# Start of a four-layer encoder: first loads in pieces of two tiles, and the squares moved behind the first value splits

## The chip, the cores and the metric

One NeuronCore of a Trainium2 chip runs the whole kernel in one launch. The metric is the device time of the launch in microseconds (us). The other cores do nothing.

## What is computed

A trunk of four layers (an even mixer, an MLP, an odd mixer, an MLP) over 256 tokens of width 1024, all in float32. Only the start of the even layer is touched by this change:

```python
def rms_norm(x, g):
    xf = x.astype(jnp.float32)
    y = xf * lax.rsqrt(jnp.mean(xf * xf, axis=-1, keepdims=True) + RMS_EPS)
    return (y * g.astype(jnp.float32)).astype(x.dtype)

xn = rms_norm(x, norm_mix[layer])
hcat = xn @ w_in                                  # 1024 -> 1952
a_qkv = hcat[..., :o0]                            # o0 = 1536: q, k, v, 512 columns each
c_q, c_kv, k_pe = 256, 128 and 32 further columns # 416 columns in all: "c" below
```

## The kernel before

`x` lies transposed in SBUF as eight tiles of 128 features by 256 tokens. The norm is applied late: the matmuls run on `x` times the gain, and their results are scaled by the reciprocal root mean square `r`, which comes from the squares of `x`. Each float32 operand is split into a high half (rounded, type fp32r) and the rest, and each product is three matmuls: high by high, high by low, low by high (`mm3`, L178).

Weights are listed in `specs` (L105 to L132) in the order of their use. Each is a `raw` tile of 128 partitions, from a pool of four (`RAWBUFS`), and its halves `whi` and `wlo` are a pair from a pool of three (`WBUFS`). `load_weight` (L137) issues a load on SP's queue, in one piece or several; `split_piece` (L152) makes a quarter of the halves, the high one with a copy on ScalarE (L175), the low one with a subtraction on VectorE (L176).

The start of the even layer runs in this order. Eight matmuls on a zero tile (`keep_warm`, L87 to L91) occupy TensorE at first. SP issues, for each k of eight, the tile k of `x` (128 KB) and the quarter of a `w_c` weight that goes with it (208 KB; `w_c` is two weights of four quarters each), then the first `w_v` weight in two pieces, the second in one, and `w_qk` (L474 to L477). The loop at L556 then does for each k: `prepare` (L224), which makes both halves of the gained tile (ScalarE L227, VectorE L228), one `split_piece`, and six matmuls of 416 columns (`c_product`). After every second k, `add_squares` (L230) squares two tiles of `x` on ScalarE (L233) and adds them up on VectorE (L235, in the end L237). Behind the loop stand the four splits of the first `w_v` weight (L569). A second part (L570 to L582) multiplies by `w_v`: `v0` and `v1` are the two token halves, four k of each with the first weight and four with the second, 12 matmuls of 512 columns each time. Between `v0` and `v1`, `rstd` (L248) sums the squares over partitions with small matmuls (L243), and `r`, `diagonal` and `c_tail` follow from it.

Both parts stand in `tc.manual_schedule`: TensorE, ScalarE and VectorE keep the written order there. The DMAs on SP keep the order in which they are written, too, and each takes the next of eight completion semaphores (`DMAHW0` to `DMAHW7` in the order listings); a DMA that takes one in use waits, on SP, until the earlier DMA has landed. `tc.issue_after(i)` puts what its block writes on the engine of the instruction `i` behind `i`; it says nothing to other engines. Behind line 582 a scheduler fills the rest of the even layer in by priorities.

Of the kernel before, what the change touches and what calls it, by code (L numbers as in the profile page):

```python
# [16 lines left out]
F32 = mybir.dt.float32  # L17
# [6 lines left out]
P = 128  # L24
D = 1024
KT = D // P
T = 256
# [7 lines left out]
WCH = 2048  # L35
# [9 lines left out]
def trunk(ctx, tc, a, out):  # L45
# [41 lines left out]
    def keep_warm(n):  # L87
        for _ in range(n):
            nc.tensor.matmul(idle, warm[:, 0:P], warm, start=True, stop=True)

    keep_warm(8)  # L91

    gains = const.tile([P, 4 * KT], F32, name="gains")
    nc.scalar.dma_start(gains, a["gains"])
    ident = const.tile([P, P], F32, name="ident")
# [41 lines left out]
    def load_weight(pieces=1, before=lambda i: None):  # L137
        j = state["loaded"]
        src, n = specs[j]
        raw = wraw.tile([P, WCH], F32, tag="raw", name="raw")  # L140
        for i in range(pieces):
            c = cut(j, i, pieces)
            before(i)
            nc.sync.dma_start(raw[:, c], src[:, c])
        parts[j] = [raw, None, None]
        state["loaded"] = j + 1
# [324 lines left out]
    def even(ep):  # L471
        xT = x_pair()
        xh, xl = halves(xT)
        for j in range(2):  # L474
            load_weight(4, lambda i: nc.sync.dma_start(x[:, 4 * j + i, :], a["x"][:, 4 * j + i, :]))
        load_weight(2)
        load_weight()  # L477
# [77 lines left out]
        with tc.manual_schedule(engines={ENG.PE, ENG.Activation, ENG.DVE}):  # L555
            for k in range(KT):  # L556
                upper, lower = prepare(k, 0, xT)
                upper()
                lower()
                split_piece()  # L560
                if k % 4 == 0:
                    wc.append(parts[k // 4][1:])
                for t in range(NT):
                    c_product(pc[t], wc[k // 4], k, t)
                if k % 2:
                    add_squares(k // 2, s)
            state["used"] = 2
            del parts[0], parts[1]
            ins = [split_piece() for _ in range(WPARTS)][-1]  # L569
        with tc.issue_after(ins[0]), tc.issue_after(ins[1]):  # L570
            with tc.manual_schedule(engines={ENG.PE, ENG.Activation, ENG.DVE}):
                v0, v1 = v_steps(0), v_steps(1)
                v0(range(4))
                small_loads()
                r = rstd(s)
                dg = [diagonal(r, t) for t in range(NT)]
                v1(range(4))
# [413 lines left out]
def _layout(i):  # L991
    f = np.ascontiguousarray
    w = i["ev_w_in"][0]
    d = {"x": f(i["x"][0][ORDER].T.reshape(KT, P, T).transpose(1, 0, 2))}
# [27 lines left out]
    gains = np.stack([i["norm_mix"], i["norm_mlp"]], 1).reshape(4 * KT, P)  # L1022
    d["gains"] = f(gains.T)
# [21 lines left out]
```

## Time and profile before

| what | us |
| --- | --- |
| median of 3 runs (lowest to highest) | 748.24 (748.11 to 748.69) |
| the profiled execution | 748.74 |
| its span, from the first to the last instruction | 747.0 |
| TensorE busy in the span | 736.6 (99%) |
| VectorE busy | 552.1 (74%) |
| ScalarE busy | 466.1 (62%) |

The profiled execution is 0.5 us over the median; 1.74 us of it lie outside the span. TensorE's busy time counts from the start of a matmul to its modelled end, so that matmuls that follow each other closely overlap, and pauses show best in the distance between starts. "PEld" is the load of the stationary operand. An entry such as `[1.78 <-DMA raw<-in_w_c]` says how long the engine had been idle and what released it.

### The profile page before, as it was taken

Reading aid. Unit: us, or ns where it says so; the run is one execution under the profiler, and the core shown is the slowest. Engines: PE = TensorE matmul, PEld = TensorE weight load, DVE = VectorE, ACT = ScalarE, POOL = GpSimd, SP = SyncE. Lnnn points to the kernel's source line nnn. Section 1 sums busy time; section 2 is a strip of 40 time slices with the busy share of each in tenths; the row PEclk is TensorE's granted clock in tenths of the full one; section 3 lists DMA queues with packets and bytes.
Section 4 is the critical chain, followed back from the end, with each engine's and each line's share of the span. In section 5 each row is a group of like instructions: output and inputs, shape, how many; then the busy total and the mean of one; then the engine's idle time right before and its main releaser. Section 6 shows DMA issues by size and latency. Waiting matters only on the chain.

```text
span 747.0 us, 12623 instructions
## 1 busy us (share of the span) xinstructions
PE 736.6 (99%) x4700; PEld 641.9 (86%) x4700; DVE 552.1 (74%) x1270; ACT 466.1 (62%) x1052; POOL 7.6 (1%) x20
## 2 busy tenths in 40 slices
PE   8999999999999999999999999999999999999996
PEld 5887899888888888989899899998998888888885
DVE  6798859766656656898988888888769665665664
ACT  6688887545545446848676867867667554554541
POOL 0100000000000000000000000000000000000000
PEclk9999999999999999999999999999999999999999
DMA  8764333655555554576555556456653655455501
GB/s 287 312 214 154 114 114 113 227 177 183 204 186 183 195 172 154 196 216 201 198 199 163 169 192 216 164 183 202 227 196 127 211 182 190 173 200 184 181 31 57
DMA packets 27421, 135.32 MB, mean 181 GB/s; under 512 B 4448, under 2 KB 7008, under 8 KB 14432
## 3 DMA queue, kind: packets, MB, share of 16 engines
q1 hardware_dynamic: 27072, 134.23, 51.9%
q8 instruction: 37, 0.61, 0.4%
q10 hardware_dynamic: 288, 0.28, 0.1%
q14 instruction: 24, 0.20, 0.1%
HBM read 127.16 MB, written 1.05 MB: 172 GB/s over the span
## 4 chain that ended last, share of the span: by engine, by line
PE 93%; DVE 2%; DMA 1%; ACT 1%; issue 1%; SPq 0%; POOLq 0%; POOL 0%; DVEq 0%
PE w L185 16%; PE acc L185 14%; PE acc L179 13%; PE acc L180 13%; PE acc L181 13%; PE w L186 8%; PE acc L186 7%; PE w L895 1%; PE w L200 1%; PE acc L910 1%; DMA raw<-in_w_v 1%; PE w L709 1%; PE w L724 1%; PE w L874 1%; DMA raw<-in_w_c 1%
## 5 line engine op out<-in xcount | busy, mean ns | idle before, releaser
L176 DVE TENSOR_TENSOR wlo<-raw,whi 128x512 fp32r<-128x512 f32 (+3 forms) x488 | 304.5, 664 | 75.2 <-ACT whi L175 73.7
L175 ACT CAST whi<-raw 128x512 fp32r<-128x512 f32 (+3 forms) x488 | 264.2, 601 | 80.6 <-issue 69.6
L185 PE MATMUL w<-xT,whi 128*128 128x512 f32 x528 | 185.1, 394 | 0.0
L185 PE MATMUL acc<-xT,whi 128*128 128x512 f32 x432 | 155.3, 402 | 0.0
L186 PE MATMUL w<-xT,wlo 128*128 128x256 f32 x528 | 137.0, 280 | 0.0
L185 PEld LDWEIGHTS w<-xT,whi 128*128 128x128 f32 x528 | 96.5, 187 | 18.8
L186 PE MATMUL acc<-xT,wlo 128*128 128x256 f32 x432 | 112.2, 280 | 0.0
L186 PEld LDWEIGHTS w<-xT,wlo 128*128 128x128 f32 x528 | 99.1, 188 | 5.7
L179 PE MATMUL acc<-whi,h 128*128 128x512 f32 x250 | 98.4, 393 | 0.0
L180 PE MATMUL acc<-wlo,h 128*128 128x512 f32 x250 | 97.8, 391 | 0.0
L181 PE MATMUL acc<-whi,h 128*128 128x512 f32 x250 | 97.4, 390 | 0.0
L185 PEld LDWEIGHTS acc<-xT,whi 128*128 128x128 f32 x432 | 78.8, 188 | 14.7
L186 PEld LDWEIGHTS acc<-xT,wlo 128*128 128x128 f32 x432 | 81.2, 188 | 4.0
L192 ACT COPY up<-w 128x256 f32<-128x256 f32 x64 | 23.9, 373 | 88.5 <-PE w L185 88.5
L193 DVE TENSOR_TENSOR up<-up,w 128x256 f32<-128x256 f32 x64 | 26.9, 420 | 62.9 <-ACT up L192 62.3
L179 PE MATMUL acc<-whi,xT 128*128 128x384 f32 (+2 forms) x160 | 56.2, 351 | 1.0 <-ACT whi L175 0.9
L180 PE MATMUL acc<-wlo,xT 128*128 128x384 f32 (+2 forms) x160 | 55.7, 348 | 0.6 <-DVE wlo L176 0.6
L181 PEld LDWEIGHTS acc<-whi,h 128*128 128x128 f32 x250 | 46.9, 188 | 10.2
L180 PEld LDWEIGHTS acc<-wlo,h 128*128 128x128 f32 x250 | 47.0, 188 | 9.8
L181 PE MATMUL acc<-whi,xT 128*128 128x384 f32 (+2 forms) x160 | 55.2, 345 | 0.0
L179 PEld LDWEIGHTS acc<-whi,h 128*128 128x128 f32 x250 | 46.9, 188 | 9.0
L180 PEld LDWEIGHTS acc<-wlo,xT 128*128 128x128 f32 x160 | 30.1, 188 | 3.2 <-DVE wlo L176 2.2
(186 smaller groups left out, 959.3 us busy)
## 6 DMA issues: line engine op xcount, KB each, us to landing
raw<-in_w SPq DMA_DIRECT2D x64, 1024.0 KB, 4.8
raw<-in_w_oqk SPq DMA_DIRECT2D x24, 1024.0 KB, 5.1
raw<-in_w_ov SPq DMA_DIRECT2D x16, 768.0 KB, 4.8
sw<-qk SPq DMA_DIRECT2D x96, 64.0 KB, 3.2
raw<-in_w_qk SPq DMA_DIRECT2D x4, 1024.0 KB, 11.0
raw<-in_w_oe SPq DMA_DIRECT2D x4, 1024.0 KB, 4.9
raw<-in_w_oo SPq DMA_DIRECT2D x4, 1024.0 KB, 5.5
bias<-in_rpb SPq DMA_DIRECT2D x8, 256.0 KB, 4.0
```

Of the source, the lines that this page charges most:

```text
L175: a = nc.scalar.copy(hi, src).ins
L176: return a, (eng or nc.vector).tensor_tensor(lo, src, hi.bitcast(F32), op=ALU.subtract).ins
L179: nc.tensor.matmul(o, sh, mh, start=first, stop=False)
L180: nc.tensor.matmul(o, sh, ml, start=False, stop=False)
L181: nc.tensor.matmul(o, sl, mh, start=False, stop=last)
L185: both = lambda: nc.tensor.matmul(o, sh, m.rearrange("p v n -> p (v n)"), start=first, stop=last)
L186: low = lambda: nc.tensor.matmul(o[:, 0:T], sl, m[:, 0, :], start=False, stop=False)
L192: nc.scalar.copy(dst, o[:, T:2 * T])
L193: nc.vector.tensor_tensor(dst, dst, o[:, 0:T], op=ALU.add)
L200: nc.tensor.matmul(o[j], qk[pb, 0, a, ts], qk[pb, 1, b, :], start=n == 0, stop=n == 2)
L709: nc.tensor.transpose(pt[:, b * P:(b + 1) * P], pp[:, b // 2, (b % 2) * P:(b % 2 + 1) * P], ident)
L724: nc.tensor.matmul(pvo[64 * j:64 * j + 64, tok(t)], v[:, kk, h * 64:(h + 1) * 64], pts[:, 2 * j + kk, :], start=kk == 0, stop=kk == NT - 1)
```

## The change

The first eight pairs of loads become seven loads. Tiles 0 and 1 of `x` come in one DMA (256 KB), then the two quarters of `w_c` for them (416 KB), then the same for tiles 2 and 3, then tiles 4 to 7 in one DMA (512 KB), then the two halves of the second `w_c` weight. The last three stand in an `issue_after` block on the seventh of now nine warm-up matmuls. The loads of the first `w_v` weight stand in `issue_after` blocks on the splits of k = 0 and 1, that of the second on the split of k = 3; `w_qk` is no longer loaded ahead by hand. The squares leave the loop: all four `add_squares` stand behind the four splits of the first `w_v` weight. `rstd` and `diagonal` move behind `v1(range(4))`. The layout of `gains` on the host stands in another place; its values are the same.

```diff
-    keep_warm(8)
+    warmed = keep_warm(9)
...
-    def load_weight(pieces=1, before=lambda i: None):
-        j = state["loaded"]
+    def load_pieces(j, i0, i1):
+
         src, n = specs[j]
-        raw = wraw.tile([P, WCH], F32, tag="raw", name="raw")
-        for i in range(pieces):
-            c = cut(j, i, pieces)
-            before(i)
-            nc.sync.dma_start(raw[:, c], src[:, c])
-        parts[j] = [raw, None, None]
-        state["loaded"] = j + 1
+        if i0 == 0:
+            parts[j] = [wraw.tile([P, WCH], F32, tag="raw", name="raw"), None, None]
+        c = slice(i0 * n // WPARTS, i1 * n // WPARTS)
+        nc.sync.dma_start(parts[j][0][:, c], src[:, c])
...
-        for j in range(2):
-            load_weight(4, lambda i: nc.sync.dma_start(x[:, 4 * j + i, :], a["x"][:, 4 * j + i, :]))
-        load_weight(2)
-        load_weight()
+        for k in (0, 2):
+            load_x(k, k + 2)
+            load_pieces(0, k, k + 2)
+        with tc.issue_after(warmed[6]):
+            load_x(4, 8)
+            load_pieces(1, 0, 2)
+            load_pieces(1, 2, 4)
+
+        def load_behind(k, done):
+
+            with tc.issue_after(done[0]):
+                if k < 2:
+                    load_pieces(2, 2 * k, 2 * k + 2)
+                elif k == 3:
+                    load_pieces(3, 0, WPARTS)
+                    state["loaded"] = 4
...
-                split_piece()
+                load_behind(k, split_piece())
                 if k % 4 == 0:
                     wc.append(parts[k // 4][1:])
                 for t in range(NT):
                     c_product(pc[t], wc[k // 4], k, t)
-                if k % 2:
-                    add_squares(k // 2, s)
...
                 v0, v1 = v_steps(0), v_steps(1)
+                for b in range(4):
+                    add_squares(b, s)
                 v0(range(4))
                 small_loads()
+                v1(range(4))
                 r = rstd(s)
                 dg = [diagonal(r, t) for t in range(NT)]
-                v1(range(4))
```

What the built program holds shows in two places. First SP's queue, from the eighth load on before, and the names of the semaphores that each waits for:

```order
L144 DMA raw<-in_w_c 128x416 [waits DMAHW0_49]
L475 DMA x<-in_x 128x256 [waits DMAHW1_49]
L144 DMA raw<-in_w_c 128x416 [waits DMAHW2_49]
L475 DMA x<-in_x 128x256 [waits DMAHW3_49]
L144 DMA raw<-in_w_c 128x416 [waits DMAHW4_49]
L475 DMA x<-in_x 128x256 [waits DMAHW5_49]
L144 DMA raw<-in_w_c 128x416 [waits DMAHW6_49]
L475 DMA x<-in_x 128x256 [waits DMAHW7_49]
L144 DMA raw<-in_w_v 128x1024 [waits DMAHW1_49]
L144 DMA raw<-in_w_v 128x2048 [waits DMAHW3_49]
L144 DMA raw<-in_w_qk 128x2048 [waits DMAHW4_49,DVE_49]
```

And SP's queue in the changed program, from the third load on:

```order
L96 DMA x<-in_x 128x512
L146 DMA raw<-in_w_c 128x832
L96 DMA x<-in_x 128x1024
L146 DMA raw<-in_w_c 128x832 x2
L146 DMA raw<-in_w_v 128x1024 [waits DMAHW0_49]
L146 DMA raw<-in_w_v 128x1024 [waits DMAHW1_49]
L146 DMA raw<-in_w_v 128x2048 [waits DMAHW2_49]
L146 DMA raw<-in_w_qk 128x2048 [waits DMAHW4_49,DMAHW3_49,DVE_49]
```

All seven loads of `x` and `w_c` now go out without a wait, and the three of `w_v` wait for the landing of the gains and of the first two loads alone. No load of `x`, `w_c` or `w_v` waits for TensorE or ScalarE: the `issue_after` blocks leave nothing on SP.

Second, VectorE from the last two k of the loop to the mean square `ms`, before:

```order
L228 SCALAR_TENSOR_TENSOR xT<-x,gains,xT 128x256
L176 TENSOR_TENSOR wlo<-raw,whi 128x416
L235 TENSOR_TENSOR squares<-squares,q 128x512
L237 TENSOR_TENSOR squares<-squares 128x256
L176 TENSOR_TENSOR wlo<-raw,whi 128x512 x8
L245 TENSOR_SCALAR ms<-w 128x2
```

And in the changed program:

```order
L232 SCALAR_TENSOR_TENSOR xT<-x,gains,xT 128x256
L180 TENSOR_TENSOR wlo<-raw,whi 128x416
L180 TENSOR_TENSOR wlo<-raw,whi 128x512 x4
L239 TENSOR_TENSOR squares<-squares,q 128x512 x3
L241 TENSOR_TENSOR squares<-squares 128x256
L180 TENSOR_TENSOR wlo<-raw,whi 128x512 x4
L249 TENSOR_SCALAR ms<-w 128x2
```

The three additions, and the one that folds the sum, now stand together between the splits of the two `w_v` weights; ScalarE's four squares moved likewise. Further on, some splits and joins change places on ScalarE and VectorE within the even layer; behind it all engines keep their order.

## Rows read from the trace of the kernel before

**Rows 1.** Chain that ended last, first 20 us (start us, us, what)
```profile
0.74 0.39 SPq L475
...
4.01 4.71 DMA raw<-in_w_c
8.74 0.38 SPq L144
9.16 6.47 DMA raw<-in_w_v
15.66 0.63 ACT whi L175
16.31 0.71 DVE wlo L176
17.06 0.50 PE acc L180
17.55 0.23 PE acc L181
```

**Rows 2.** Timeline, first products (start us, us, engine, line, names, shapes, [idle <-releaser])
```profile
1.19 3.47 PE L89 MATMUL acc<-warm 128*128 128x512 bf16 x8 [1.19 <-DVE warm L84]
...
4.15 0.53 ACT L175 CAST whi<-raw 128x416 fp32r<-128x416 f32 x1
...
4.74 0.45 PE L179 MATMUL acc<-whi,xT 128*128 128x416 f32 x1
...
5.36 0.45 PE L180 MATMUL acc<-wlo,xT 128*128 128x416 f32 x1 [0.17 <-DVE wlo L176]
...
7.47 0.45 PE L179 MATMUL acc<-whi,xT 128*128 128x416 f32 x1 [0.90 <-ACT whi L175]
...
8.57 0.35 PE L179 MATMUL acc<-whi,xT 128*128 128x416 f32 x1
...
8.76 0.35 PE L180 MATMUL acc<-wlo,xT 128*128 128x416 f32 x1
```

**Rows 3.** Timeline of VectorE, one pair of tiles in the loop
```profile
8.38 0.49 DVE L228 SCALAR_TENSOR_TENSOR xT<-x,gains,xT 128x256 fp32r<-128x256 f32 x1 [0.34 <-ACT xT L227]
...
10.22 0.69 DVE L235 TENSOR_TENSOR squares<-squares,q 128x512 f32<-128x512 f32 x1
10.82 0.48 DVE L228 SCALAR_TENSOR_TENSOR xT<-x,gains,xT 128x256 fp32r<-128x256 f32 x1
...
15.73 0.42 DVE L237 TENSOR_TENSOR squares<-squares 128x256 f32<-128x256 f32 x1
```

**Rows 4.** DMA share and GB/s by stretch (last two columns; the first is the stretch)
```profile
1.50:4.70 3.20, 3.16 (x8) 0.91 (x6) 0.42 (x1) 2.12 (x5) 0.00 (x0) 1.00 0.79 199
4.70:7.50 2.80, 1.69 (x7) 1.08 (x7) 1.05 (x4) 1.02 (x3) 0.00 (x0) 1.00 0.90 279
7.50:9.50 2.00, 1.83 (x8) 1.24 (x8) 1.66 (x4) 2.00 (x5) 0.00 (x0) 1.00 1.06 340
9.50:13.00 3.50, 3.50 (x18) 3.27 (x19) 3.50 (x8) 3.50 (x9) 0.00 (x0) 1.00 0.84 264
13.00:16.40 3.40, 3.40 (x19) 3.08 (x18) 3.21 (x8) 2.30 (x6) 0.00 (x0) 1.00 1.01 405
16.40:20.00 3.60, 3.37 (x17) 2.57 (x16) 2.50 (x4) 2.03 (x4) 0.00 (x0) 1.00 1.00 423
```

**Rows 5.** Timeline of SP: DMAs issued
```profile
4.96 0.43 SPq L144 DMA_DIRECT2D raw<-in_w_c  x1
5.44 0.43 SPq L475 DMA_DIRECT2D x<-in_x  x1
6.87 0.33 SPq L144 DMA_DIRECT2D raw<-in_w_c  x1
...
7.84 0.33 SPq L144 DMA_DIRECT2D raw<-in_w_c  x1
```

**Rows 6.** DMAs issued at 1.19, 2.12 and 7.84 us: KB, us to landing
```profile
raw<-in_w_c SPq DMA_DIRECT2D x1, 208.0 KB, 2.9
...
raw<-in_w_c SPq DMA_DIRECT2D x1, 208.0 KB, 4.7
...
raw<-in_w_c SPq DMA_DIRECT2D x1, 208.0 KB, 4.5
```

**Rows 7.** TensorE's waits from 4 us to the end (total us, times, longest)
```profile
PE acc L179 <- ACT whi L175: 0.9, 1, 0.9
PE acc L179 <- DVE oa L176: 0.7, 1, 0.7
PE acc L180 <- DVE wlo L176: 0.6, 3, 0.2
PE w L615 <- DVE mn L694: 0.5, 1, 0.5
```

**Rows 8.** Timeline of VectorE, late in the even layer's first heads
```profile
56.26 0.69 DVE L711 COPY pts<-w 128x512 f32<-128x512 f32 x1 [0.52 <-PE w L709]
...
58.85 0.69 DVE L711 COPY pts<-w 128x512 f32<-128x512 f32 x1 [1.16 <-PE w L709]
```

More of the change, by code (lines that the diff above doesn't have):

```diff
@@ L87, in keep_warm, with load_x @@
     def keep_warm(n):
-        for _ in range(n):
-            nc.tensor.matmul(idle, warm[:, 0:P], warm, start=True, stop=True)
-    keep_warm(8)
+        return [nc.tensor.matmul(idle, warm[:, 0:P], warm, start=True, stop=True).ins for _ in range(n)]
+    warmed = keep_warm(9)
     gains = const.tile([P, 4 * KT], F32, name="gains")
     nc.scalar.dma_start(gains, a["gains"])
+    def load_x(k0, k1):
+        nc.sync.dma_start(x[:, k0:k1, :], a["x"][:, k0:k1, :])
     ident = const.tile([P, P], F32, name="ident")
@@ L135, in trunk, with load_weight @@
     state = {"loaded": 0, "split": 0, "used": 0}
-    def load_weight(pieces=1, before=lambda i: None):
-        j = state["loaded"]
+    def load_pieces(j, i0, i1):
         src, n = specs[j]
-        raw = wraw.tile([P, WCH], F32, tag="raw", name="raw")
-        for i in range(pieces):
-            c = cut(j, i, pieces)
-            before(i)
-            nc.sync.dma_start(raw[:, c], src[:, c])
-        parts[j] = [raw, None, None]
-        state["loaded"] = j + 1
+        if i0 == 0:
+            parts[j] = [wraw.tile([P, WCH], F32, tag="raw", name="raw"), None, None]
+        c = slice(i0 * n // WPARTS, i1 * n // WPARTS)
+        nc.sync.dma_start(parts[j][0][:, c], src[:, c])
+    def load_weight():
+        load_pieces(state["loaded"], 0, WPARTS)
+        state["loaded"] += 1
     def cut(j, i, n):
@@ L993, in _layout @@
     w = i["ev_w_in"][0]
-    d = {"x": f(i["x"][0][ORDER].T.reshape(KT, P, T).transpose(1, 0, 2))}
+    gains = np.stack([i["norm_mix"], i["norm_mlp"]], 1).reshape(4 * KT, P)
+    d = {"x": f(i["x"][0][ORDER].T.reshape(KT, P, T).transpose(1, 0, 2)), "gains": f(gains.T)}
     d["w_c"] = f(w[:, 1536:].reshape(2, 4, P, 416).transpose(0, 2, 1, 3).reshape(2, P, -1))
@@ L1021, in _layout @@
     d["norm_final"] = f(i["norm_final"])
-    gains = np.stack([i["norm_mix"], i["norm_mlp"]], 1).reshape(4 * KT, P)
-    d["gains"] = f(gains.T)
     return d
```

## The prediction

> **What bounds the kernel now.** I read the page first: TensorE is busy for 99% of the span, and the view of waits says that from 4 us to the end it waits about 3 us in all [rows 7]. What this change can give is therefore small and lies where TensorE is not yet fed, at the start. There I read the chain that ended last [rows 1]: it runs over SP's issues, a load of `w_c`, SP again, a load of `w_v`, a split on ScalarE, its other half on VectorE, and reaches TensorE at 17.06; from there it is TensorE on and on. So the end is set by when TensorE gets into its stride, and a microsecond won before 17 us should be one at the end.
>
> Next the timeline. The first product starts at 4.74, 0.59 us behind the high split at 4.15; its second matmul, at 5.36, stands 0.43 us later than an undisturbed one would, whose distance is 0.19 us (8.57 to 8.76) [rows 2]. The product of k = 1 starts at 7.47 only, because its quarter of `w_c` came late. The loop holds 8 x 6 = 48 matmuls, 48 x 0.19 = 9.1 us; the value matmuls begin at about 16.8 (the one at 17.06, less one distance of 0.23 as in [rows 1]). From 4.74 to 16.8 are 12.1 us, so some 3 us are lost.
>
> Three things end together at 16 us. VectorE takes 10.82 - 8.38 = 2.44 us for a pair of k, squares included, against 12 x 0.19 = 2.28 on TensorE, and has its last sum at 15.73 [rows 3]. The first `w_v` piece lands at 15.6 [rows 1]. And TensorE itself is hardly ahead of either. Taking away one limit alone would give nothing; the change touches all three.
>
> **The change part by part.** The profiled execution took 748.74 us, 0.5 over the median, with 1.74 outside the span. All differences below are inside the span, so I take them from the median, 748.24.
>
> *Squares out of the loop.* VectorE loses 0.60 us per pair (10.22 to 10.82), and then needs 2.44 - 0.60 = 1.84, less than TensorE's 2.28; ScalarE loses as much. The loop is then paced by TensorE and by the loads. The work is not gone: 3 x 0.60 + 0.42 = 2.2 us now stand on VectorE between the splits of the two `w_v` weights. TensorE has 24 value matmuls with the first weight, 24 x 0.23 = 5.5 us, before it needs the second; the squares (2.2) and four splits (4 x 0.63, from the 0.71 of one in [rows 1], which overlap) take 4.7 on VectorE, which starts them before TensorE is through the loop. Hidden. Queued behind them are `ms`, `r` and the tail of c. If that is late, VectorE is late in the first heads; there it has 0.52 + 1.16 = 1.7 us of waiting for TensorE [rows 8], which is the cover. I cost it at nothing, and at up to 2.2 - 1.7 = 0.5 us if VectorE is not ahead at all.
>
> *Later `rstd`.* Its two small matmuls move 12 value matmuls (2.8 us) back on TensorE. `ms` stood behind eight splits on VectorE anyway. Nothing.
>
> *The ninth warm-up matmul.* Eight take 3.47 us, so one takes 0.43 and the ninth ends near 5.1. That is before the first product as I place it below (6.2), so it costs nothing; if the data came as early as before (4.74), it would cost 0.4.
>
> *SP's queue.* The load of the sixth quarter was issued at 6.87, 1.43 us behind the one before, where SP otherwise issues every 0.47 [rows 5]: it waited for a semaphore in use. Now no load of `x` or `w_c` waits, and at 0.47 us each all are issued by 4.0, the `w_v` loads by about 6. The blocks "behind" the warm-up matmul and the splits leave no wait on SP, as the order shows, so what holds is the plain order of the queue. While SP had stopped, the DMA engines still had work, but the share falls to 0.84 in 9.5 to 13 us, at 264 GB/s [rows 4]. I expect that gap to close.
>
> *First pieces twice as large.* This is the price. The first product needs 256 + 416 = 672 KB to have landed, where 336 KB did before. Low bound: 336 KB had landed at 1.19 + 2.9 = 4.1 [rows 6]; 336 KB more (0.34 MB) at the best pace of the neighbourhood, 423 GB/s [rows 4], is 0.8 us: 4.9. High bound: before, the same 672 KB were there when the second quarter landed, at 2.12 + 4.7 = 6.8 [rows 6]. I take 5.6: nearer the low end, since the same bytes come in two loads rather than four and nothing else is asked of the queue. First product at 5.6 + 0.6 = 6.2; with the 0.43 and 9.1 us of matmuls the loop ends at 15.7 (15.0 to 16.9 by the bounds).
>
> *Tiles 4 to 7 ahead of their weights.* k = 4 now needs all 1024 KB of `x` and six quarters of `w_c`, 2272 KB (2.33 MB). Before, 2352 KB had landed at 7.84 + 4.5 = 12.3 [rows 5, 6]: high bound. Low bound: 2.33 MB at 405 GB/s from 1.5 us on is 5.8 us, plus about 1 us to land: 8.3. Between them stands the stretch in which the queue was full with just these short rows, 340 GB/s [rows 4]: 6.9 us from 1.5, plus 1.3 lost in the slow first stretch (3.2 us at 199 instead of 340), plus some 0.8 us from last byte to landing: 10.5. Product of k = 4 at 10.5 + 0.6 = 11.1, then 0.43 + 24 x 0.19 = 5.0: the loop ends at 16.1.
>
> *Values.* At 340 GB/s the rest of `w_c` and the first half `w_v` (928 KB) have landed by 13.3, and are split before 15; the 0.4 us that TensorE lost at 17.06 go.
>
> The loop ends between 15.7 and 16.1 by the two paths; I take 16.0, against 16.8 before: 0.8 us won. 748.24 - 0.8 = 747.4.
>
> **A rule beside the row.** Rows of 1.0 to 1.7 KB per partition moved at 199 to 340 GB/s, those of `w_v` and `w_qk` (4 and 8 KB) at 405 to 423 [rows 4]. The Trainium skill, "DMA: Bandwidth & Descriptors", section "Specifications", gives 512 B as the size from which a transfer runs at line rate; by that, rows of 1 KB lose nothing, longer ones win nothing, and the old pace by bytes would hold (the second rival below). The trace speaks against it as far as longer rows and higher rates stand together, though the stretches differ in more than the rows.
>
> **The rivals.** *Loads at the pace of the long rows.* If 405 GB/s held from the start, both low bounds apply, the loop ends at 15.0, and 1.8 us are won: 746.4. For it: rows grow to 2, 3.3 and 4 KB. Against it: the first stretch, 199 GB/s at a share of 0.79, which is a start and not a matter of rows.
>
> *The old pace by bytes.* Then k = 4 waits for 12.3 less 0.3 us (80 KB at 264 GB/s), the loop ends at 12.0 + 0.6 + 5.0 = 17.6, and 0.8 us are lost: 749.0. For it: the share of 0.79 to 1.06 says the DMA engines were mostly busy, not starved. Against it: the 0.84 behind SP's stop.
>
> *A cold TensorE (slower).* Between the ninth warm-up matmul (5.1) and the first product TensorE has nothing. With the high bound the product starts at 7.4, a pause of 2.3 us. The longest pause before was 0.90, up to 7.47, and the granted clock read 1.00 around it [rows 2, 4]. If the clock falls to its lower level, as in the warm-up matmuls (0.43 us for 512 columns against 0.23 for the value ones), the way back took some 3.5 us at the start (1.19 to 4.74), half of which is lost: 1.75. The loop ends at 16.9 + 1.75 = 18.7: 1.9 us lost, 750.1. It decides if the product starts over 2 us behind the warm-up.
>
> *The change doesn't do what it says.* It doesn't, as to the two kinds of "behind" on SP; the order shows it and the sums above have it in. It gives no time of its own.
>
> **How the numbers follow.** Forecast (0 to 1.6 us won, 746.6 to 748.2): 0.62. Fast loads: 0.17. Old pace: 0.14. Cold TensorE: 0.05; late tail of c beyond its cover (748.7 at most): 0.02. The 8 in 10 reach from 746.3 (fast rival) to 749.0 (old pace), leaving out what lies past 749.0 (0.13) and below 746.3 (0.07). A measurement of this kernel tells about 0.2%, 1.5 us, from no change: faster than 746.7 is most of the fast rival, 0.16, and the edge of the forecast, 0.09: 0.25. Slower than 749.7: the cold case and the tail of the old pace, 0.07. The same: 0.68.
>
> **What would show it.** In the profile of the changed kernel: no SP issue of `x` or `w_c` with a gap over 0.5 us; the first product near 6.2 (under 5.6: fast rival; over 7.2: late); from k = 0 to k = 3 distances of 0.19 with at most one pause before k = 2; a pause before k = 4, with the release by a `w_c` load, and the first value matmul near 16.0; no wait between the two matmuls there; the granted clock at 1.00 from 5 us on. The forecast is wrong if the pause before k = 4 is over 1 us, or if the value matmuls start earlier by some amount and the `pts` copies near 58 us by clearly less: then the gain was lost in the first heads.

## The result: 2.3 us slower, and where they go

The changed kernel takes 751.11 us (median of 11 runs, 749.48 to 752.63) against 748.84 us for the kernel before (11 runs, 748.11 to 749.43): a ratio of 1.0027, 95% interval 1.0019 to 1.0035. The interval lies above 1, so it is slower, by 0.3%; the prediction was 747.4, with 0.07 for slower. The profiled execution of the changed kernel took 751.11 us (span 749.2), that of before 748.74 (747.0).

One correction to the section on the kernel before: L474 to L477 load the two `w_c` and the two `w_v` weights (the first `w_v` in two pieces, the second in one). Neither kernel loads `w_qk` by hand there.

To see where the time goes I paired the TensorE instructions that stand in the same order in both traces and took the difference of their starts, the *delay*. It is +2.04 us at the first product, +0.83 at the second value matmul (17.06 in the kernel before), +0.68 at 23 us of the kernel before, +0.75 at 41, +1.76 at 46.8, +2.35 at 53, and from 56 us to the end +2.2. So there are three losses, and all are over by 56 us: about 0.8 at the start, 1.0 between 41 and 47 us, 0.4 between 47 and 56.

### The profile page after: what moved, and what is told of

Its sections match the earlier page's. It is cut to its first block, busy times and chain, and to the rows that moved or that the text cites. A ratio compares the mean times of both kernels' runs of the same rounds, so it can differ in the third digit from the quotient of the medians.

```text
span 749.2 us, 12608 instructions
## 1 busy us (share of the span) xinstructions
PE 738.3 (99%) x4701; PEld 643.9 (86%) x4701; DVE 552.1 (74%) x1270; ACT 466.0 (62%) x1052; POOL 8.0 (1%) x20
## 3 DMA queue, kind: packets, MB, share of 16 engines
HBM read 127.16 MB, written 1.05 MB: 171 GB/s over the span
## 4 chain that ended last, share of the span: by engine, by line
PE 91%; DVE 4%; issue 2%; ACT 1%; DMA 1%; POOL 1%; POOLq 0%; SPq 0%; DVEq 0%
PE w L189 16%; PE acc L183 13%; PE acc L184 13%; PE acc L185 13%; PE acc L189 13%; PE w L190 8%; PE acc L190 6%; DVE wlo L180 1%; PE w L912 1%; PE w L204 1%; PE acc L927 1%; PE w L726 1%; PE w L741 1%; PE w L891 1%; DMA raw<-in_w_c 1%
## 5 line engine op out<-in xcount | busy, mean ns | idle before, releaser
L183 PEld LDWEIGHTS acc<-whi,xT 128*128 128x128 f32 x160 | 30.6, 191 | 3.3 <-ACT whi L179 2.5
```

Source lines behind the costliest of these rows:

```text
L183: nc.tensor.matmul(o, sh, mh, start=first, stop=False)
```

## The profile after

**The start.** The timeline of TensorE, which answers to [rows 2] (start us, us, engine, line, names, shapes, [idle <-releaser]):

```profile
1.19 4.02 PE L88 MATMUL acc<-warm 128*128 128x512 bf16 x9 [1.19 <-DVE warm L84]
...
4.57 0.63 PE L88 MATMUL acc<-warm 128*128 128x512 bf16 x1
6.77 0.72 PE L183 MATMUL acc<-whi,xT 128*128 128x416 f32 x1 [1.56 <-ACT whi L179]
...
8.95 0.55 PE L185 MATMUL acc<-whi,xT 128*128 128x416 f32 x1
9.30 0.55 PE L183 MATMUL acc<-whi,xT 128*128 128x416 f32 x1
...
10.74 0.35 PE L185 MATMUL acc<-whi,xT 128*128 128x416 f32 x1
10.93 0.35 PE L183 MATMUL acc<-whi,xT 128*128 128x416 f32 x1
...
17.66 0.39 PE L183 MATMUL acc<-whi,xT 128*128 128x512 f32 x1
17.89 0.39 PE L184 MATMUL acc<-wlo,xT 128*128 128x512 f32 x1
```

The first product comes at 6.77. Its successors stand 0.35 us apart (8.95, 9.30), and from about 10.5 us 0.19 apart (10.74, 10.93). For 416 columns these are the two clock levels, 1.2 and 2.4 GHz. Between the warm-up matmuls and the first product TensorE has a pause of 1.56 us, and behind it nearly two tiles of k run at the lower level; before, the distance was 0.19 from 8.57 on [rows 2]. In this execution the level had not been up at all: from 1.19 to the ninth warm-up matmul at 4.57 they stand 0.42 apart, and the ninth still takes 0.63 (the second line is from a narrower window of the same view). The first two value matmuls stand at 17.66 and 17.89; before, they stood at 16.43 and, held up for its split, 17.06.

DMA by stretch, the same stretches as [rows 4] (last three columns: granted clock, DMA share, GB/s):

```profile
1.50:4.70 3.20, 3.20 (x9) 1.06 (x7) 0.00 (x0) 1.60 (x3) 0.00 (x0) 1.00 0.78 214
4.70:7.50 2.80, 1.24 (x4) 0.39 (x2) 1.23 (x3) 1.39 (x5) 0.00 (x0) 1.00 1.03 349
7.50:9.50 2.00, 2.00 (x6) 1.92 (x7) 1.69 (x5) 1.59 (x5) 0.00 (x0) 1.00 1.01 402
9.50:13.00 3.50, 3.50 (x18) 3.45 (x18) 3.04 (x8) 2.95 (x8) 0.00 (x0) 1.00 1.05 420
```

The loads do what the change wants: 214, 349, 402 and 420 GB/s where before had 199, 279, 340 and 264. No product waits for data behind the first one. (The clock column reads 1.00 here even where the distances show the lower level; the distances decide.) So the 0.8 us are not the loads' fault as a whole, but their first piece's: it is there later, and the pause ahead of it leaves TensorE at the lower level. What each of the two costs is read from e2 below.

**The first heads.** The chain that ended last, which answers to [rows 1] (start us, us, what):

```profile
1.18 4.98 DMA raw<-in_w_c
6.18 0.55 ACT whi L179
...
23.44 0.35 PE w L247 x4
24.13 0.72 POOL rstd L255
...
25.87 1.89 DVE wlo L180 x3
...
46.90 0.47 DVE qk L180
47.61 0.52 ACT pp L719
48.17 0.84 PE w L726 x4
```

Before, the chain ran over TensorE alone from 17 us on. Now it leaves TensorE at the small matmuls of `rstd` (23.44) and runs over GpSimd's `rstd` and VectorE's `wlo` splits until it comes back at 48.17: for 25 us VectorE and its helpers, not TensorE, set the pace. Of VectorE's timeline, the changed kernel first, then the instruction of before that answers to its first row:

```profile
23.81 0.16 DVE L249 TENSOR_SCALAR ms<-w 128x2 f32<-128x2 f32 x1 [1.71 <-PE w L247]
...
51.00 0.42 DVE L711 CUSTOM_DVE_ANT_0 sn<-w,bias 128x256 f32<-128x256 f32 x1 [0.77 <-PE w L204]
...
58.42 0.69 DVE L728 COPY pts<-w 128x512 f32<-128x512 f32 x1 [0.83 <-PE w L726]
61.02 0.69 DVE L728 COPY pts<-w 128x512 f32<-128x512 f32 x1 [1.16 <-PE w L726]
```

```profile
22.58 0.15 DVE L245 TENSOR_SCALAR ms<-w 128x2 f32<-128x2 f32 x1
```

`ms` now waits 1.71 us for the sums over partitions, because their matmuls stand behind `v1`; it comes 1.2 us later than before, where it did not wait at all. The four splits of the next weight stand behind it on VectorE, in order. The delay reaches TensorE, which before has no such wait, in the first heads (TensorE, changed kernel):

```profile
42.52 0.50 PE L204 MATMUL w<-qk 64*128 64x256 f32 x4 [0.37 <-DVE qk L180]
```

The `pts` copies at 58 and 61 us still wait 0.83 and 1.16, where [rows 8] has 0.52 and 1.16: that idle time was not used up.

## The experiments

Each kernel was run beside the kernel before on the same chip; "+1.63" is the difference of the two medians. The delays in this table are from one profiled execution each. That the two controls of the last group (g2, h3), whose first 40 us should be those of before, read -0.48 and -0.05 throughout says how far such a reading scatters.

| kernel | at 17 | 23 | 41 | 46.8 | 53 | 70 us | medians |
| --- | --- | --- | --- | --- | --- | --- | --- |
| changed | +0.83 | +0.68 | +0.75 | +1.76 | +2.35 | +2.18 | +2.27 |
| e1 | +1.22 | +1.15 | +1.15 | +1.15 | +1.68 | +1.53 | +1.63 |
| e2 | -0.60 | -0.75 | -0.68 | +0.33 | +0.92 | +0.77 | +1.70 |
| e3 | -0.59 | +0.11 | +0.11 | +0.11 | +0.64 | +0.48 | +0.77 |
| e4 | +0.02 | -0.04 | +0.88 | +1.14 | +1.14 | +1.17 | +1.21 |
| e5 | +0.40 | +0.31 | +0.32 | +0.31 | +0.85 | +0.67 | +1.62 |
| e6 | +0.51 | +4.48 | +4.52 | +4.52 | +5.06 | +4.90 | +4.67 |
| e7 | +0.95 | +0.79 | +1.20 | +1.24 | +1.24 | +1.26 | +0.71 |
| e10 | +0.43 | +0.35 | +0.35 | +0.57 | +1.16 | +1.00 | +0.83 |
| f4 | -0.47 | -0.55 | -0.55 | -0.41 | +1.48 | +1.32 | +1.67 |
| g1 | -0.62 | -0.77 | -0.63 | -0.15 | +1.44 | +1.27 | +1.34 |
| h1 | -0.58 | -0.73 | -0.61 | -0.24 | +0.35 | +0.18 | +0.19 |

### The two suspects: e1, e2, e3

e1 moves `rstd` back between `v0` and `v1`, in the changed kernel:

```diff
-                v1(range(4))
                 r = rstd(s)
                 dg = [diagonal(r, t) for t in range(NT)]
+                v1(range(4))
```

> The changed kernel with rstd and diagonal put back in front of v1(range(4)); all else as changed. Theory (two losses): the changed kernel loses some 0.7 us up to the value matmuls and another 1.5 us because the mean square ms stands on VectorE ahead of the w_qk splits and waits 1.71 us for the moved small matmuls of rstd. Put back, that wait goes: VectorE's ms waits less than 0.3 us, TensorE keeps its delay from 23 us to the end, and the time falls by about 1.5 us, to some 0.7 us over the kernel before (0.1%). Rival (the order of splits and joins that the scheduler chose for the first heads costs the 1.5 us): no change against the changed kernel, some 2 us over before (0.27%).

Measured: 750.31 us (749.57 to 750.67), ratio 1.0021 [1.0012, 1.0030]; 0.64 less than the change. `ms` does not wait, and the step of 1.0 between 41 and 47 us is gone from the table; the median gained less than the 1.5 us expected, and this profile began 0.4 us later at 17 us. The start is not mended; its profile shows another way to the lower level (TensorE):

```profile
4.57 0.46 PE L88 MATMUL acc<-warm 128*128 128x512 bf16 x1
6.93 0.45 PE L183 MATMUL acc<-whi,xT 128*128 128x416 f32 x1 [1.90 <-ACT whi L179]
...
7.86 0.35 PE L185 MATMUL acc<-whi,xT 128*128 128x416 f32 x1
8.04 0.46 PE L183 MATMUL acc<-whi,xT 128*128 128x416 f32 x1
...
8.64 0.55 PE L185 MATMUL acc<-whi,xT 128*128 128x416 f32 x1
8.99 0.55 PE L183 MATMUL acc<-whi,xT 128*128 128x416 f32 x1
```

The first products are 0.18 apart (7.86 to 8.04), and from about 8.3 us 0.35: the level had been up and fell behind a pause of 1.90 us. Here the ninth warm-up matmul takes 0.46, where it took 0.63 in the changed kernel, and the view by stretch reads a granted clock of 0.50 from 9 to 10.5 us.

e2 keeps TensorE at work until the data come, in the changed kernel:

```diff
-    warmed = keep_warm(9)
+    warmed = keep_warm(14)
```

> The changed kernel with 14 warm-up matmuls in place of 9. Theory (clock): in the changed kernel's profile the first ten products stand 0.35 us apart, later ones 0.19: TensorE ran at the lower of its two levels up to 10.4 us, since it stood still from 5.1 to 6.8 us. With 14 warm-ups it is busy until the data come, nearly all 48 products stand 0.19 us apart from the first on, the loop ends near 16.3 in place of 17.7, and 1.0 to 1.4 us are won against the changed kernel; the runs lie closer together (their range was 3.1 us). Rival (late data alone): the products start at 6.8 as before and are held up for data anyway, so the loop ends at 17.7 whatever the level, and nothing is won.

Measured: 750.38 us (749.53 to 751.03), ratio 1.0020 [1.0011, 1.0029]. TensorE:

```profile
1.19 5.37 PE L88 MATMUL acc<-warm 128*128 128x512 bf16 x14 [1.19 <-DVE warm L84]
6.71 0.45 PE L183 MATMUL acc<-whi,xT 128*128 128x416 f32 x1
...
7.62 0.35 PE L185 MATMUL acc<-whi,xT 128*128 128x416 f32 x1
7.81 0.35 PE L183 MATMUL acc<-whi,xT 128*128 128x416 f32 x1
```

With the first product at the same time (6.71 for 6.77) and a pause of only 0.15 ahead, the distances are 0.19 from 7.62 on, and the second value matmul comes 0.60 us *earlier* than before instead of 0.83 later: the lower level cost 1.4 us in these two executions, and the late first piece by itself did not put the values behind those of before. But the 0.75 us in hand at 23 us are gone by 46.8 (+0.33): `rstd` is still late. From column to column the two rows of the table stay 1.4 apart (1.43 at 17 us, 1.41 at 70): what the start won went through to the end in full, and the late `rstd` and the heads took their share on top. The medians differ by less, 0.57.

e3 is both edits:

> Both edits: 14 warm-up matmuls, and rstd and diagonal in front of v1(range(4)). Theory (two losses that add up): 2.5 to 2.9 us under the changed kernel, that is 0.3 to 0.8 us under the kernel before (0.05 to 0.1% faster). Rival (they overlap, since VectorE's wait would be hidden by a start that comes earlier): no more than the better of the two single edits.

Measured: 749.45 us (748.91 to 750.27), ratio 1.0011 [1.0002, 1.0020]. The two edits take 1.5 of the 2.27 us away, but the kernel is not under before, as it was expected to be. Left are 0.7 us between 17 and 23 us, where the small matmuls of `rstd` now wait 0.53 for the squares, and a step at 50 us that no reason of mine had covered.

### The parts of the change: e4, e5, e6, e7

e4 keeps all of the change but the loads:

```diff
-        for k in (0, 2):
-            load_x(k, k + 2)
-            load_pieces(0, k, k + 2)
...
+        for k in range(8):
+            load_x(k, k + 1)
+            load_pieces(k // 4, k % 4, k % 4 + 1)
```

> The changed kernel with the loads of before: single tiles with single quarters, all w_v loads issued behind them in one go; 9 warm-up matmuls, squares behind the value splits and rstd behind v1(range(4)) as changed. Theory: the first product is back at 4.7 to 5.1, the products stand 0.19 us apart, the semaphore wait on SP is back; the loop ends at 16.0 to 16.4, limited by late quarters of w_c. The loss by the late rstd stays: some 1.5 us over before, or 1.2 if the start wins a little. Rival (the new loads are the whole loss): as fast as before.

Measured: 749.89 us (748.89 to 750.47), ratio 1.0013 [1.0004, 1.0022]. Nothing is lost at the start, 0.9 by 41 us; there is no step at 50 us.

e5 keeps only the loads and the ninth warm-up matmul (squares in the loop, `rstd` between `v0` and `v1`):

```diff
                     c_product(pc[t], wc[k // 4], k, t)
+                if k % 2:
+                    add_squares(k // 2, s)
...
-                for b in range(4):
-                    add_squares(b, s)
```

> The new loads and 9 warm-up matmuls alone: squares back in the loop, rstd in front of v1(range(4)). Theory (the start loses by its first product and by the clock): first product at 6.2 to 6.9, its neighbours 0.35 us apart for 3 to 5 us, the loop ends at 17.2 to 18.3 since VectorE needs 2.44 us a pair on top; 0.6 to 1.5 us are lost up to the values, and 0.3 more in the first heads, where the scheduler has another order: 0.9 to 1.8 us over before (0.12 to 0.24%). Rival (the loads cost nothing by themselves, only together with the moved squares): within 0.3 us of before.

Measured: 750.33 us (749.20 to 751.54), ratio 1.0020 [1.0011, 1.0028]. The start again runs at the lower level, until 9.7 us behind a pause of 1.29; its profiled execution, the third fastest of eleven at 749.84, lost less (+0.67) than the median run (+1.62).

e6 keeps only the squares behind the splits (loads as before in e4, `rstd` as in e1):

> The moved squares alone: loads of before (single tiles), rstd in front of v1(range(4)), 9 warm-up matmuls. Theory: the loop is rid of 0.6 us per pair on VectorE but the quarters of w_c then end it, at 16.0 to 16.4; TensorE waits some 0.5 us for the squares at rstd's small matmuls, as in the run with both edits; 0.3 us go in the first heads. In all 0.2 to 0.8 us over before (0.03 to 0.1%). Rival (VectorE was the bound of the loop, as forecast): 0.5 us or more under before.

Measured: 753.38 us (751.43 to 755.10; 6 runs), ratio 1.0058 [1.0044, 1.0071]. I had expected far less. TensorE:

```profile
22.58 0.58 PE L247 MATMUL w<-mean,squares 128*128 128x1 f32 x4 [2.18 <-DVE squares L241]
...
24.46 0.63 PE L185 MATMUL acc<-whi,xT 128*128 128x512 f32 x1
24.89 0.63 PE L183 MATMUL acc<-whi,xT 128*128 128x512 f32 x1
...
27.45 0.40 PE L183 MATMUL acc<-whi,xT 128*128 128x512 f32 x1
27.68 0.40 PE L184 MATMUL acc<-wlo,xT 128*128 128x512 f32 x1
```

The squares stand behind the splits of the first `w_v` weight on VectorE; with the loads of before these come later, and `rstd` stops TensorE for 2.18 us. Behind the stop the level falls: 0.43 us for 512 columns (24.46 to 24.89) up to 27.4, then 0.23. The delay goes from +0.51 to +4.48: the stop, and eight matmuls at 0.20 us more. So with the loads of before, moving the squares forbids an early `rstd`; with the new ones an early `rstd` is the better choice (e1, e3).

e7 is the kernel before with the late `rstd` alone:

> The kernel before with one edit: rstd and diagonal behind v1(range(4)). VectorE's order is that of before to the last instruction. Theory (ms heads VectorE's queue and waits for the moved matmuls, and the w_qk splits wait behind it): VectorE's ms waits 0.5 to 1.0 us, the tail of c comes later by as much, TensorE keeps its times up to 36 us and is 0.7 to 1.2 us late from 60 us on; 749.4 to 749.9 beside 748.7. Rival (it is the scheduler's other order of the heads that costs it): within 0.2 us of before.

Measured: 749.42 us (748.29 to 750.01), ratio 1.0008 [1.0000, 1.0017]. `ms` waits 1.05 us here too. In its profile 0.95 us of the delay are from the start, where this execution had a pause of 1.45 us ahead of k = 1 and the lower level behind it; 0.4 arise between 23 and 41 us, which is what the late `rstd` did without the moved squares beside it.

### Mending all at once: f1, f2, e10, f3, f4

f1 is the kernel before with two warm-up matmuls for eight, f2 the kernel before with four more in the pause behind k = 0:

> The kernel before with 2 warm-up matmuls in place of 8; all else, and the order on every engine, as before. It prices TensorE's level by itself. Theory (clock): TensorE stands still from 2.0 to 4.7 us, the products begin at 4.74 as before but 0.35 us apart up to 8 to 11 us; 12 of them take 4.2 us a pair of k where VectorE needs 2.44, so the loop ends 1.0 to 2.0 us later, the whole is 0.8 to 1.8 us slower (749.5 to 750.5), and the runs spread further. Rival (the start is bound by the loads, not by TensorE): within 0.3 us of before.

> The kernel before with four more warm-up matmuls behind the products of k = 0, where TensorE waits for the second quarter of w_c (6.4 to 7.5 us); the order elsewhere as before. Theory: they fit into the pause (4 x 0.22 = 0.9 us) and TensorE's level, once up, doesn't fall; the median falls by 0 to 0.4 us and the runs lie closer together than the 1.4 us of before. Rival: the pause was too short to matter, or the four matmuls end late and push k = 1 back: 0 to 0.3 us slower.

Measured: f1 749.28 us (748.71 to 749.70), ratio 1.0005 [0.9996, 1.0014]; f2 748.80 us (748.25 to 749.41), ratio 1.0000 [0.9992, 1.0009]. In f1 the products run at the lower level up to 9.8 us, and yet the profile loses only 0.3 us and the median 0.6, within the noise. By my reading the loop waits for loads and VectorE there anyway, so that a slow start is dear only where the loads are ahead, as the change makes them. f2 shows that the lower level needs no pause (TensorE):

```profile
4.15 0.63 PE L89 MATMUL acc<-warm 128*128 128x512 bf16 x1
4.77 0.71 PE L179 MATMUL acc<-whi,xT 128*128 128x416 f32 x1
...
6.26 0.55 PE L179 MATMUL acc<-whi,xT 128*128 128x416 f32 x1
6.60 0.55 PE L180 MATMUL acc<-wlo,xT 128*128 128x416 f32 x1
```

The eighth warm-up matmul ends where the first product starts, and the products still stand 0.35 apart: the level comes up later, near 7.0 us. Up to here f2 is the kernel before, whose own profile has distances of 0.19 in the first tile (5.65 to 5.84). So when the level comes up differs between executions.

e10 is the changed kernel with tiles 0 and 1 as single loads, ten warm-up matmuls and `rstd` in the middle of `v1`:

```diff
-            load_x(k, k + 2)
-            load_pieces(0, k, k + 2)
+        for k in (0, 1):
+            load_x(k, k + 1)
+            load_pieces(0, k, k + 1)
...
-                v1(range(4))
+                v1(range(2))
                 r = rstd(s)
                 dg = [diagonal(r, t) for t in range(NT)]
+                v1(range(2, 4))
```

> A version meant to win: the changed kernel, but tiles 0 and 1 with their quarters as four single loads as before, 10 warm-up matmuls, and rstd in the middle of v1(range(4)), behind two of its k. Theory: first product at 4.9 to 5.6, the level up by 5.6, the loop ends at 15.6 to 16.2, ms waits less than 0.4 us, no wait for the squares; 0.6 to 1.0 us won up to the values, 0.3 to 0.6 lost again in the first heads: 0 to 0.7 us under before. Rival (whatever is won at the start goes in the heads, where VectorE and ScalarE are the bound): as before or slower.

Measured: 749.54 us (749.30 to 749.77), ratio 1.0011 [1.0002, 1.0019], the narrowest of all. It was built to win and did not. Neither `ms` nor the squares are waited for; 0.6 us of its delay arise between 46.8 and 53 us.

f3 has the loads of before, the fill of f2, half of the squares in the loop and `rstd` in the middle of `v1`:

> A version meant to win: loads of before, the four filling matmuls, the squares of tiles 0 to 3 in the loop as before and those of tiles 4 to 7 behind the first value splits, rstd in the middle of v1(range(4)). VectorE and TensorE have the order of before from the first heads on. Theory: VectorE is rid of 1.2 us in the second half of the loop, which then ends by its loads at 15.9 to 16.3, no wait for the squares over 0.3 us, nothing lost in the heads: 0.2 to 0.6 us under before. Rival (the loads and the first w_v piece, at 15.6, hold the values where they were): within 0.2 us of before.

Measured: 749.24 us (749.03 to 750.15), ratio 1.0009 [1.0000, 1.0018], no win either: its profile is 0.2 us ahead at 23 us and 0.2 behind at 53, lost mostly between 23 and 41 us.

f4 is e2 with `rstd` in the middle of `v1`:

> The changed kernel with 14 warm-up matmuls and rstd in the middle of v1(range(4)). Theory: as the run with 14 warm-ups and rstd in front (749.45 beside 748.68), without its 0.5 us wait for the squares at rstd's matmuls; values start 0.6 to 1.1 us earlier than before, ms waits less than 0.4 us; what is left is lost in the first heads by the other order there: 748.7 to 749.3, still not under before. Rival (the heads' order costs nothing): 748.0 or less.

Measured: 750.34 us (749.09 to 751.56), ratio 1.0021 [1.0012, 1.0030], a miss: it was to show that the two suspects are all. It is 0.55 us ahead up to 41 us, and 1.48 behind at 53. VectorE:

```profile
50.51 0.42 DVE L712 CUSTOM_DVE_ANT_0 sn<-w,bias 128x256 f32<-128x256 f32 x1 [2.44 <-DMA bias<-in_rpb]
```

### The third loss, at 47 to 53 us: g1 to g4, h1, h3

The bias (`rpb`) of an item of the attention is loaded when the buffer two items before it is free. SP's timeline of f4 (the `w_oe` here is its second), then of before, where the second comes behind the bias:

```profile
42.47 0.33 SPq L146 DMA_DIRECT2D raw<-in_w_oe  x1
44.09 0.33 SPq L692 DMA_DIRECT2D bias<-in_rpb  x1
```

```profile
39.94 0.33 SPq L144 DMA_DIRECT2D raw<-in_w_oe  x1
44.16 0.33 SPq L674 DMA_DIRECT2D bias<-in_rpb  x1
46.06 0.33 SPq L144 DMA_DIRECT2D raw<-in_w_oe  x1
```

The scheduler has put two `w_oe` weights ahead of the third bias where before had one; the same flip is in the changed kernel, e1, e2, e3, e5, e6 and e10, and in none of e4, e7 and f3. My first theory was the queue: a bias behind a weight. g1 is f4 with these biases issued by GpSimd, which is idle there; the order on TensorE, VectorE and ScalarE is f4's:

```diff
-                nc.sync.dma_start(biases[n], a["rpb"][t, hp])
+                (nc.sync if n < 2 else nc.gpsimd).dma_start(biases[n], a["rpb"][t, hp])
```

> The kernel of f4 (changed kernel, 14 warm-ups, rstd between the halves of the second value group), with the attention's bias loads from the third on issued by GpSimd instead of the SP queue; the order of instructions on TensorE, VectorE and ScalarE is that of f4. Theory: what f4 lost at 47 to 53 us (from 0.41 us ahead to 1.48 us late) is VectorE's wait of 2.44 us for a bias that stood behind a weight load on the SP queue. Then that wait goes, the delay at 53 us is at most 0.5, and the time falls from 750.3 to 748.7 to 749.3. Rival: the loss is the scheduler's other order of splits and joins, which this leaves alone; then the wait for the bias turns into one for something else and the time stays at 750.0 to 750.6.

Measured: 750.03 us (749.22 to 750.50), ratio 1.0015 [1.0006, 1.0024]. The theory of the queue fell. GpSimd's issue, then VectorE:

```profile
44.62 0.72 POOL L692 DMA_DIRECT2D bias<-in_rpb  x1 [9.91 <-DVE mn L712]
```

```profile
50.49 0.42 DVE L712 CUSTOM_DVE_ANT_0 sn<-w,bias 128x256 f32<-128x256 f32 x1 [2.17 <-DMA bias<-in_rpb]
```

The bias is issued as soon as its buffer is free, on a queue of its own, and still is not there before 50.5. The view of DMA issues gives its way from issue to landing (KB, us), of this third bias in before, f4 and g1:

```profile
bias<-in_rpb SPq DMA_DIRECT2D x1, 256.0 KB, 3.1
```

```profile
bias<-in_rpb SPq DMA_DIRECT2D x1, 256.0 KB, 6.3
```

```profile
bias<-in_rpb POOLq DMA_DIRECT2D x1, 256.0 KB, 5.7
```

Twice as long, on either queue. What differs from before is the second `w_oe` weight, 1024 KB, asked for 1.6 us ahead of the bias in f4 (42.47 to 44.09): before, the last weight ahead of it was asked for 4.2 us earlier (39.94 to 44.16). The Trainium skill, "DMA: Bandwidth & Descriptors", section "Issuing engines are not separate DMA queues", says that transfers issued by any engine run on the same 16 DMA engines and interleave there; 5.7 against 6.3 us agrees.

g2, g3 and g4 are the same edit in the kernel before, in the changed kernel and in e3:

> The kernel before with the same edit alone, as the control. Before, no instruction of the first heads waits over 0.3 us for a bias, so both theories expect the time of before within 0.3 us (748.4 to 749.0). If this gains clearly (0.5 us or more), the edit is worth something by itself and the gain of g1 is no proof for the place of the bias load.

> The changed kernel with the same edit alone. Its order on the SP queue differs from before too (two w_oe loads ahead of a bias), but its one long wait there (0.77 us on VectorE at 51 us) is put down to a matmul. If that is really the bias: 750.3 to 750.7 from 751.1. If it is the matmul, as the row says: 750.9 to 751.3, since the start's clock and the late rstd stay.

> The kernel of e3 (changed kernel, rstd early, 14 warm-ups; 749.45 us, of which the profile lost 0.4 us in the first heads) with the same edit. If those 0.4 us are the bias: 749.0 to 749.2; if they are the order on the engines: 749.3 to 749.6. Either way it is not expected below 748.8, the kernel before.

Measured: g2 748.49 us (748.20 to 749.67), ratio 1.0002 [0.9993, 1.0010]; g3 751.24 us (751.00 to 751.40, 5 runs), ratio 1.0035 [1.0022, 1.0049]; g4 749.49 us (749.16 to 749.78), ratio 1.0011 [1.0003, 1.0020]. No effect: in the changed kernel and in e3 the bias is not what is late.

h1 is f4 with the bias in single heads, five buffers of half the size, so that half of the third bias is loaded before the weights; again in f4's order on the engines. h3 is the control on the kernel before:

```diff
-                biases[n] = ep.tile([P, 2, T], F32, tag="bias", name="bias", bufs=2)
-                nc.sync.dma_start(biases[n], a["rpb"][t, hp])
+                biases[i] = ep.tile([P, T], F32, tag="bias", name="bias", bufs=5)
+                nc.sync.dma_start(biases[i], a["rpb"][t, hp][:, i % 2])
```

> The kernel of f4 with the bias cut into single heads of 128x256: five buffers of half the size in place of two (1 KB a partition more), five loads ahead of the attention, so that one half of the third bias is there before the w_oe weights are asked for. Order on TensorE, VectorE and ScalarE as in f4. In g1 the third bias was issued at 44.6 us, at once when its buffer was free, and landed 5.9 us later, beside w_oe weights that load at 260 to 320 GB/s; before, the second of these weights is asked for only behind it (46.1 us), and it lands in time. Theory: the loss at 47 to 53 us is this slow landing. Then the wait of 2.2 to 2.4 us falls under 0.8, the delay at 53 us is at most +0.2, and the time is 748.3 to 749.2, from 750.0 to 750.3. Rival: the order of splits and joins costs it whatever the bias does; then 749.7 to 750.4 and a wait for something else in its place.

> The control: the kernel before with the same edit alone. No VectorE instruction of its first heads waits for a bias, so both theories expect 748.4 to 748.9. A gain of 0.5 us or more here would mean that the cut of the bias is worth something by itself.

Measured: h1 749.05 us (748.50 to 749.45), ratio 1.0002 [0.9994, 1.0011]; h3 748.91 us (748.65 to 750.06), ratio 1.0001 [0.9992, 1.0010]. The edit is worth 1.5 us in f4 by the medians, each against its own before, 1.1 by the profiles, and nothing in before, so the late bias was most of f4's third loss. VectorE of h1, in its place:

```profile
49.00 0.42 DVE L712 CUSTOM_DVE_ANT_0 sn<-w,bias 128x256 f32<-128x256 f32 x1 [0.77 <-PE w L204]
```

This wait of 0.77 us is the one that the changed kernel has at 51.00. Every kernel of the table with the two `w_oe` weights in a row has a step of about 0.5 us between 50 and 53 us (f4 and g1 more, by the bias), of which 0.2 come back by 56; those without have none. In h1 two quarter splits of 128x256 stand on VectorE ahead of the second item's scores (at 45.81), where before has them behind (at 47.60); so behind the `pts` copy at 47.17 it has nothing left to do but wait for the next scores. That the flipped order causes the step is an inference from the table; I did not put the old order into the changed kernel.

h1 is the change with the losses mended as far as I could: no slower than before by its interval, and not faster. Its profile was 0.58 us ahead at 17 us; 0.4 of that go by 46.8 us and the step of 0.5 takes the rest.

## Why the prediction was wrong, step by step

The steps that failed are two terms set at nothing: the late `rstd`, which took 1.0 us, and the ninth warm-up matmul with the pause behind it, which took 1.4 us in the profiles. A third loss of 0.4 us, in the heads, had no term.

*What bounds the kernel.* "A microsecond won before 17 us should be one at the end" held as far as it goes: changed kernel and e2 stay 1.4 us apart from 17 us to the end, and g2, which has the order of before, was 0.47 us early at 17 us in its profile and 0.45 at 70. What failed is that only the start was counted: the change also delays work that TensorE needs at 41 to 48 us. Of the kernel before, 36 to 52 us (the stretch and its length, then busy us of PE, PEld, VectorE and the others):

```profile
36.00:52.00 16.00, 16.00 (x103) 13.32 (x102) 15.91 (x48) 13.72 (x38) 0.19 (x1) 1.00 0.57 198
```

VectorE is busy for 15.91 of 16 us, so there is next to no room in which it could catch up. "TensorE on and on" was true of the chain and hid that VectorE has as little slack.

*Faster loads, squares out of the loop: right.* Once under way the loads moved 349 to 420 GB/s where the sum took 340, SP did not stop, k = 4 did not wait: its weights, issued at 3.06, took 7.6 us to land, 10.7 for the forecast's 10.5. (The 0.8 us from last byte to landing in that sum, and the 1 us of its low bound, stand on no row.) In e2 the second value matmul comes 0.60 us early; the forecast was 0.8. The Trainium skill, "DMA: Bandwidth & Descriptors", section "Specifications", has the line rate from 512 B on, by which the old pace by bytes would have stayed; the 402 and 420 GB/s where before had 340 and 264 speak against it again, though the end of SP's stop is in that gain too.

*First pieces: late by half a microsecond.* I took 5.6 for the landing of the second load, between 4.9 and 6.8; the split that it releases starts at 6.18, and the first product came at 6.77 for 6.2. The rest of that path was right where the level was up: in e2, 6.71 + 0.43 + 9.1 = 16.24 us, and the first value matmul stands at 16.23. (The 16.8 of before, against which the 0.8 was counted, is its second value matmul less one distance; its first stood at 16.43, and the wait of 0.4 between the two has gone, as forecast.)

*The cold TensorE: right cost, wrong condition and chance.* I had the level up by the end of the warm-up, to fall in a pause of "over 2 us", and put 0.05 on it. In the changed kernel's profile it had not come up in the nine warm-up matmuls, so it had nothing to fall from. Where it was up first, pauses of 1.45 (e7) and 1.90 us (e1) had the lower level behind them, and the 0.90 of before did not [rows 2]. The forecast's own 6.2, with the last warm-up matmul ending at 5.1, already asked for a pause of 1.1. The ninth warm-up matmul, costed at nothing, was too few. The price of the lower level, 1.75 by my sum, is 1.4 between the profiles of the changed kernel and e2; between their medians, each against its own before, it is 2.27 - 1.70 = 0.57. That some executions pay less would explain this and is not shown.

*"Later `rstd`: Nothing."* This failed. `ms` stood behind eight splits before, as I said, but so closely that 12 value matmuls (2.8 us) more could not be hidden: it waits 1.71 us, four splits queue behind it, and TensorE falls 1.0 us back at 41 to 47 us. Putting `rstd` back takes that step away in both pairs; by the medians it gives 0.64 (e1), with the clock mended 0.93 (e2 to e3).

*The cover.* I counted the 1.7 us that VectorE waits at 56 and 59 us as cover [rows 8]. It lies behind the place where the delay has to be caught up: TensorE waits for VectorE's work at 42.52, and the waits at 58 and 61 are no shorter in the changed kernel. "Squares hidden" depends on `rstd`: with an early one they stop TensorE for 0.53 (e3) or 2.18 us (e6), and the late one alone cost 0.4 (e7), with the squares moved 1.0. The two moves are one decision, and I priced them apart.

*The heads.* The step of about 0.4 us from the other order of weights and splits is in no term. The last paragraph of the prediction named the sign by which it would show (a gain at the start, less at the `pts` copies), but gave it no chance.

By the profile the sum is: start +0.83, up to 41 us -0.08, `rstd` +1.01, heads and the rest +0.46: 2.22 us. With the clock mended the start is -0.60, and 1.43 of the sum is the lower level. What remains open is how the start is shared out over executions (the medians of the changed kernel and e2 differ by less than half of what their profiles do), what makes the scheduler flip the order of the weights, and whether that flip is what costs the 0.4 us in the heads.

## What to carry to other kernels

Idle time covers a delay only if it lies between the place of the delay and the place where the delayed result is due; look for the first instruction queued behind the moved one, not for idle time on the engine somewhere later. When first loads are made larger, the engine that is kept warm for them has to be kept warm longer, up to the first product and not up to where it used to be; read from the distances whether it was warm by then at all. And look at the scheduler's order behind a hand-written stretch too: a prefetch that it moves ahead of a small load can double the small load's way, whichever queue issues it.

## What the runs showed of the hardware

In e7, e1 and e6 TensorE was at the upper level, paused for 1.45, 1.90 and 2.18 us, and was at the lower level behind it; in e1 and e6 the first products behind the pause still ran at the upper one. In e6, in the middle of dense work, one stop of 2.18 us cost 4.0 us in all. In the changed kernel the level had not come up by the end of nine warm-up matmuls, and it was up only at 10.5 us, behind a pause of 1.56. Its twin at the start, g3, reads the same: first distance of 0.19 behind 10.58, +0.82 at 17 us.

A load of 256 KB took 3.1 us to land beside one weight of 1024 KB issued 4.2 us earlier, and 6.3 us beside one issued 1.6 us earlier on the same queue (f4); on another queue, with the weight some 1.9 us ahead, it took 5.7 (g1).

The same program's start is not the same in every execution: e7 has the instructions of before up to 17 us and had its pause ahead of k = 1 at 1.45 us in the profile, where before had 0.90, and e1 has those of the changed kernel and ended its warm-up at the upper level. The changed kernel's runs spread over 3.2 us, those of e10, whose first loads are small again, over 0.5.
